# The opening of a two-layer trunk: where the first norm's sums are added up, and in which order the first steps stand

## The chip, the core and the metric

The kernel runs on one core of a Trainium2 chip. The metric is the device time of one execution in microseconds (us), lower is better. A core has five engines that run side by side, each through its own list of instructions: TensorE (PE; its weight loads are shown apart, as PEld), VectorE (DVE), ScalarE (ACT), GpSimd (POOL) and SyncE (SP), which here only issues DMA transfers. TensorE multiplies a stationary operand, loaded first, by a moving one, and adds up in PSUM banks; the other operands lie in SBUF.

## The reference, cut to what matters

The program is a trunk of two layers over 256 latent tokens and 256 context tokens of width 1024. Layer 0 has attention (a differential and a grouped-query part) and a gated feed-forward part, layer 1 a state-space mixer and a feed-forward part. The change touches only the way into layer 0:

```python
def rms_norm(x, g):
    x32 = x.astype(jnp.float32)
    y = x32 * lax.rsqrt(jnp.mean(x32 * x32, axis=-1, keepdims=True) + NORM_EPS)
    return (y * g.astype(jnp.float32)).astype(x.dtype)

def modulate(x, g, shift, scale):
    return rms_norm(x, g) * (1.0 + scale) + shift
...
        mod = jax.nn.silu(c) @ mod_w[layer] + mod_b[layer]
        mod_c = jax.nn.silu(c_ctx) @ mod_w[layer] + mod_b[layer]
        sh1, sc1, g1, sh2, sc2, g2 = jnp.split(mod[:, None, :], 6, axis=-1)
...
        h = modulate(x, norm_mix_g[layer], sh1, sc1)
        hc = modulate(ctx, norm_mix_g[layer], sh1c, sc1c)
...
    qa, ka, va, qb, kb, vb = jnp.split(h @ w_in, ATTN_SPLITS, axis=-1)
```

Before the first projection `h @ w_in` can start, the kernel needs one reciprocal root for each token and, for each channel, a shift and a scale out of the modulation `silu(c) @ mod_w`.

## The kernel before, in words

**Tiling.** Activations lie transposed: `self.x[k]`, k = 0 to 7, holds 128 channels by 512 tokens (256 latent, 256 context). Projections work in steps: `gemm_step` takes one 128x128 block of weights and issues three matmuls over 512 tokens, high part by high, high by low and low by high (L289, L290, L291), since both operands are split in two so as to keep fp32 accuracy. Weights come in units of eight blocks (512 KB); `take` hands out the next unit and `feed` keeps the loads going: `load_raw` (L244) issues the DMA on SP's queue into one of five `raw` buffers, and `split_one` copies the high part on ACT (L232) and subtracts it on POOL (for `ai`, the first projection) or DVE (L234) into one of two `ws` buffers. Modulation weights use the same `raw` buffers without a split. The order of all units is fixed by `plan`: at the start two halves of a modulation piece (`mod_s`), as many `ai` units as the next k needs, and so on. So a later load waits until an earlier unit has been used.

**The start.** SP issues the first parameters, the eight `x` pieces, constants, and then units. POOL writes constants (L622 to L632). ACT computes silu of the conditioning vectors (L635) into `cpad`, then runs a one-element Sqrt (L637), which brings that function's table in ahead of its use. In `attention`, PE first runs `spin`: matmuls over a zero tile whose results nobody reads, 30 of them. ACT squares each `x[k]` (L677); DVE and POOL add the eight squares up in two running sums (L680). `rstd_of` sums each of the two over channels on PE (`token_sums`, L504), adds the results on DVE (L542, L543), and `rsqrt` takes the reciprocal root with one correction step (L509 to L519). Between that and `spread` (L523), which copies each token's value over all partitions with matmuls, stands `fill`: the first modulation piece and spins.

**A modulation piece.** `mod_start(k, h)` multiplies one half of piece k (L451, four matmuls on four groups of 32 columns); `mod_fold(k)` copies the sums (L458), folds the four groups together on PE (L460) and writes shift and scale on DVE (L463, L465). `make_h(k)` then builds both halves of `h[k]`: the product on DVE (L561, tile `ht`), the high part on ACT (L563), the low part on DVE (L568).

**The loop behind it.** For each k, six blocks of `ai` are accumulated in six banks, and among them stand the two halves of piece k + 1, its fold, and `make_h(k + 1)`. At k = 0 the halves stand apart, with spins and one step between. Tile's scheduler orders the instructions of each engine, but those passed to `pin` (spins, modulation matmuls, folds, and here the spread) stay in program order among themselves. `SPIN` holds the numbers of spins at the seven places.

Of the kernel before, what the change touches and what calls it, by code (L numbers as in the profile page):

```python
# [11 lines left out]
F32 = mybir.dt.float32  # L12
BF16 = mybir.dt.bfloat16
F32R = mybir.dt.float32r
AF = mybir.ActivationFunctionType
ALU = mybir.AluOpType
# [4 lines left out]
P = 128  # L21
D = 1024
KD = 8
# [5 lines left out]
EPS = 1e-6  # L29
# [109 lines left out]
class Trunk:  # L139
# [124 lines left out]
    def drain(self):  # L264
        while self.queue:
            _, fn = self.queue.popleft()
            fn()


    def gemm_step(self, g):  # L270
# [314 lines left out]
    def normed_start(self, phase, g, n, l, cs):  # L585
        self.mod_flush()
        self.feed(self.n_use)
        ps = g.ps[0] = g.bank(f"{g.name}0")
        r = self.rows(self.rstd_of(self.nparts, n, D, fill=lambda: self.spin(ps, SPIN[5]), preload=AF.Gelu))
        self.spin(ps, SPIN[6])  # L590
        self.pinned = True
# [9 lines left out]
    def run(self):  # L601
        nc = self.nc
        self.plan()
        with self.pool("const") as cp, self.pool("small") as sp, self.pool("raw", bufs=RAW_BUFS) as rp, \
                self.pool("wsplit") as wp, self.pool("psum", space=PSUM) as pp:
            self.constp, self.smallp, self.rawp, self.splitp, self.psump = cp, sp, rp, wp, pp
            self.prm_t = cp.tile([P, NPRM], F32, name="prm")
            self.cst_t = cp.tile([P, 386], F32, name="cst")
            self.fold = self.cst_t[:, 384:386]
            self.ident = self.cst("ident")  # L610
            self.x = [cp.tile([P, 512], F32, name=f"x{k}") for k in range(KD)]
            self.h = [cp.tile([P, 2, 512], F32R, name=f"h{k}") for k in range(KD)]
            with self.tc.high_priority(PRIO):
                nc.sync.dma_start(out=self.prm_t[:, 0:128], in_=self.a["prm"][:, 0:128])
                for k in range(KD):
                    nc.sync.dma_start(out=self.x[k], in_=self.a["x"][k])
                nc.sync.dma_start(out=self.cst_t, in_=self.a["cst"][:, 0:386])
                for _ in range(3):
                    self.load_raw()
                nc.sync.dma_start(out=self.prm_t[:, 128:], in_=self.a["prm"][:, 128:])  # L620
            self.zero = cp.tile([P, P], BF16, name="zero")
            nc.gpsimd.memset(self.zero, 0.0)  # L622
            self.modT = [cp.tile([P, 48, 2], F32, name=f"modT{l}") for l in range(2)]
            self.cpad = cp.tile([P, KD, 32], F32, name="cpad")
            self.eps = cp.tile([P, 1], F32, name="eps")
            nc.gpsimd.memset(self.cpad, 0.0)
            nc.gpsimd.memset(self.eps, EPS)
            self.warm = cp.tile([P, 1], F32, name="warm")
            self.pick = cp.tile([P, 2, 32], F32, name="pick")
            nc.gpsimd.memset(self.pick, 0.0)  # L630
            for t in range(2):
                nc.gpsimd.memset(self.pick[:, t, t:t + 1], 1.0)  # L632
            self.modb1 = cp.tile([P, KD], F32, name="modb1")
            nc.vector.tensor_scalar(out=self.modb1, in0=self.prm("modb")[:, 8:16], scalar1=1.0, scalar2=None, op0=ALU.add)
            nc.scalar.activation(out=self.cpad[:, :, 0:2], in_=self.prm("c").rearrange("p (k t) -> p k t", t=2),  # L635
                                 func=AF.Silu)
            nc.scalar.activation(out=self.warm, in_=self.cpad[:, 0, 0:1], func=AF.Sqrt, scale=0.0, bias=self.eps)  # L637
            self.attention()
            self.ffn(0, 512, "f0i", "f0o")
            self.ssm()  # L640
            self.ffn(1, 256, "f1i", "f1o")
            self.final()


    def attention(self):
        nc, cp = self.nc, self.constp
        with self.pool("at") as ap:
# [21 lines left out]
            first = [self.bank(t, f"ai{m}") for m, t in enumerate(tags)]  # L669
            g.bank = lambda name: first.pop(0)  # L670
            self.mod_ps = self.bank("mod", "modps")
            self.spin(first[5], SPIN[0])
            acc = [ap.tile([P, 512], F32, tag="qf", bufs=3, name="xacc") for i in range(2)]
            for k in range(KD):
                sq = acc[k] if k < 2 else self.smallp.tile([P, 512], F32, tag="nacc" if k in (4, 7) else "sq",
                                                           bufs=1 if k in (4, 7) else 2, name="sq")
                nc.scalar.activation(out=sq, in_=self.x[k], func=AF.Square)  # L677
                if k >= 2:
                    o = k % 2 if k < 7 else 0
                    (nc.gpsimd if o else nc.vector).tensor_tensor(out=acc[o], in0=acc[o], in1=sq, op=ALU.add)  # L680

            def fill():
                for h in range(2):
                    self.mod_start(0, h)
                self.spin(first[5], SPIN[1])
                self.mod_fold(0)
                self.spin(first[5], SPIN[2])

            ps = self.rows(self.rstd_of(acc[::-1], 512, D, True, fill))
            self.spin(first[5], SPIN[3])  # L690
            self.make_h(0, (0, 1), 0, 1, ps)
            for k in range(KD):
                while len(g.held) * UB < 6 * (k + 1) - g.pos - (-g.pos) % UB:
                    g.held.append(self.take())
                if k + 1 < KD:
                    self.mod_start(k + 1, 0)
                    if k == 0:
                        self.spin(first[5], SPIN[4])
                        self.gemm_step(g)
                    self.mod_start(k + 1, 1)  # L700
                    for _ in range(2):
                        self.gemm_step(g)
                    self.mod_fold(k + 1)
                    self.make_h(k + 1, (0, 1), 0, 1, ps)
                while g.pos < 6 * k + 6:
                    self.gemm_step(g)
# [594 lines left out]
PRIO2 = 10  # L1301
FIRST = 7
LAM_AT = 6
SPIN = (30, 4, 0, 4, 2, 4, 4)
RAW_BUFS = 5
RAW_AHEAD = 3
SPLIT_BUFS = 2
# [91 lines left out]
```

## Time and profile before

| | |
|---|---|
| time, median of 3 runs | 1190.23 us (1189.91 to 1192.31) |
| the profiled execution's own time | 1190.27 us |
| its span, first to last instruction | 1188.5 us |
| PE busy | 1160.5 us, 98% of the span |
| DVE / ACT / POOL busy | 826.6 / 604.1 / 88.9 us |
| mean granted TensorE clock | 0.987 |
| first `ai` matmul (L289) | 21.55 us after the start |

Times in the views are us from the first instruction. In a timeline row stand start, duration, engine, line, operation, what it writes and reads, and how many were merged into the row; in brackets the idle time before it and what ended it. In the chain of waits a row is a piece of the chain that ended last. In a row of stretches stand its bounds, its length, PE's busy time and number of instructions, the granted clock as a share of full speed, the share of DMA time, and GB/s. A busy PE is not PE at its peak: a matmul over two columns is shown as busy while weights for the next are loaded.

### The profile page before, as it was taken

To read this page: it belongs to the slowest core of one execution; us is meant where nothing else is said; L and a number is where in the kernel's file an instruction comes from. 1 tells how busy PE (TensorE), PEld (TensorE's weight loads), DVE (VectorE), ACT (ScalarE), POOL (GpSimd) and SP (SyncE) were. 2 spreads that over 40 slices of the span, in tenths; PEclk is the share of its full clock that TensorE was granted. 3 is DMA by queue.
4 is the path that set the end of the run, shared out by engine and by line. 5 is a ranking of instruction groups with operands and counts; after the bars stand their busy time and mean duration, and the time that the engine had idled before them with its cause. 6 is when DMAs were issued, how large, how long until landed. Compare 5 with 4: busy or idle time off the path is not lost.

```text
span 1188.5 us, 17744 instructions
## 1 busy us (share of the span) xinstructions
PE 1160.5 (98%) x6902; PEld 950.5 (80%) x6902; DVE 826.6 (70%) x1341; ACT 604.1 (51%) x1072; POOL 88.9 (7%) x67
## 2 busy tenths in 40 slices
PE   8999999999999999999999998899999999999997
PEld 4765566668988888888888997787878898999997
DVE  3569756744767786855566468799999767877654
ACT  3266656543633333333223276777877546555542
POOL 2332112200000000000000000011111101000000
PEclk8999999999999999999999998899999999999998
DMA  8633133332255454644576232554545356776651
GB/s 294 236 132 107 53 107 107 107 107 79 81 155 165 140 186 135 188 131 146 179 242 230 73 105 96 147 146 119 141 127 125 104 183 188 234 216 217 184 182 54
DMA packets 56932, 176.67 MB, mean 149 GB/s; under 512 B 6096, under 2 KB 15888, under 8 KB 56848
## 3 DMA queue, kind: packets, MB, share of 16 engines
q1 hardware_dynamic: 56272, 175.01, 47.5%
q8 instruction: 54, 0.88, 0.3%
q10 hardware_dynamic: 576, 0.52, 0.1%
q14 instruction: 30, 0.25, 0.1%
HBM read 174.40 MB, written 1.11 MB: 148 GB/s over the span
## 4 chain that ended last, share of the span: by engine, by line
PE 88%; DVE 7%; ACT 2%; DMA 2%; issue 1%; POOL 0%; DVEq 0%; SPq 0%; ACTq 0%; POOLq 0%
PE f0i L289 6%; PE f0i L290 6%; PE f0i L291 6%; PE si L289 4%; PE f1i L290 4%; PE f1i L291 4%; PE f1i L289 4%; PE si L291 3%; PE si L290 3%; PE f0o L289 3%; PE f0o L290 3%; PE f0o L291 3%; PE ai L289 3%; PE ai L291 2%; PE ai L290 2%; PE y L1255 2%
## 5 line engine op out<-in xcount | busy, mean ns | idle before, releaser
L232 ACT ACTIVATE ws<-raw 128x1024 fp32r<-128x1024 f32 x215 | 227.1, 1056 | 264.8 <-PE f0i L291 91.3
L234 DVE TENSOR_TENSOR ws<-raw,ws 128x1024 fp32r<-128x1024 f32 x197 | 240.7, 1222 | 101.8 <-ACT ws L232 100.4
L289 PE MATMUL f0i<-h,ws 128*128 128x512 f32 x336 | 131.4, 391 | 0.0
L290 PE MATMUL f0i<-h,ws 128*128 128x512 f32 x336 | 130.9, 389 | 0.0
L291 PE MATMUL f0i<-h,ws 128*128 128x512 f32 x336 | 130.8, 389 | 0.0
L289 PE MATMUL si<-h,ws 128*128 128x256 f32 (+1 forms) x312 | 112.0, 359 | 3.7 <-DVE cacc L1019 3.7
L409 DVE SCALAR_TENSOR_TENSOR macc<-raw,cpad,macc 128x1024 f32<-128x1024 f32 x70 | 89.2, 1281 | 32.8 <-DMA raw<-mod_w 32.6
L291 PE MATMUL si<-h,ws 128*128 128x256 f32 (+1 forms) x312 | 107.0, 343 | 0.5 <-DVE ws L234 0.4
L290 PE MATMUL si<-h,ws 128*128 128x256 f32 (+1 forms) x312 | 106.6, 342 | 0.0
L290 PE MATMUL f1i<-h,ws 128*128 128x256 f32 x352 | 99.6, 283 | 0.3 <-DVE h L568 0.3
L289 PE MATMUL f1i<-h,ws 128*128 128x256 f32 x352 | 99.4, 284 | 0.3 <-ACT h L563 0.3
L291 PE MATMUL f1i<-h,ws 128*128 128x256 f32 x352 | 99.5, 283 | 0.0
L289 PEld LDWEIGHTS f0i<-h,ws 128*128 128x128 f32 x336 | 63.1, 188 | 14.3 <-ACT hid L573 0.8
L291 PEld LDWEIGHTS f0i<-h,ws 128*128 128x128 f32 x336 | 63.1, 188 | 13.2
L290 PEld LDWEIGHTS f0i<-h,ws 128*128 128x128 f32 x336 | 63.1, 188 | 12.8
L289 PEld LDWEIGHTS si<-h,ws 128*128 128x128 f32 x312 | 60.6, 194 | 14.8 <-issue 9.3
L289 PEld LDWEIGHTS f1i<-h,ws 128*128 128x128 f32 x352 | 67.3, 192 | 1.2 <-ACT h L563 0.7
L290 PEld LDWEIGHTS f1i<-h,ws 128*128 128x128 f32 x352 | 67.6, 192 | 0.5 <-DVE h L568 0.5
L291 PEld LDWEIGHTS f1i<-h,ws 128*128 128x128 f32 x352 | 67.6, 192 | 0.0
L291 PEld LDWEIGHTS si<-h,ws 128*128 128x128 f32 x312 | 60.4, 193 | 7.4 <-DVE ws L234 1.1
L290 PEld LDWEIGHTS si<-h,ws 128*128 128x128 f32 x312 | 60.7, 195 | 5.5
L289 PE MATMUL ai<-h,ws 128*128 128x512 f32 x144 | 62.5, 436 | 0.1
(293 smaller groups left out, 2668.4 us busy)
## 6 DMA issues: line engine op xcount, KB each, us to landing
raw<-mod_w SPq DMA_DIRECT2D x80, 512.0 KB, 3.7
raw<-w_f0i SPq DMA_DIRECT2D x44, 512.0 KB, 4.1
raw<-w_f1i SPq DMA_DIRECT2D x44, 512.0 KB, 4.2
raw<-w_si SPq DMA_DIRECT2D x41, 512.0 KB, 3.7
raw<-w_f0o SPq DMA_DIRECT2D x22, 512.0 KB, 4.6
raw<-w_f1o SPq DMA_DIRECT2D x22, 512.0 KB, 3.6
raw<-w_ai SPq DMA_DIRECT2D x18, 512.0 KB, 3.9
raw<-mod_s SPq DMA_DIRECT2D x16, 512.0 KB, 4.7
```

The source lines that it names most:

```text
L232: ops = [nc.scalar.activation(out=hi, in_=r, func=AF.Copy)]
L234: ops.append(eng.tensor_tensor(out=s[:, 1].rearrange("p a b -> p (a b)"), in0=r, in1=hi.bitcast(F32), op=ALU.subtract))
L289: nc.tensor.matmul(ps, lhsT=s[:, 0, b], rhs=xh[:, 0:n], start=first, stop=False)
L290: nc.tensor.matmul(ps, lhsT=s[:, 0, b], rhs=xl[:, 0:n], start=False, stop=False)
L291: nc.tensor.matmul(ps, lhsT=s[:, 1, b], rhs=xh[:, 0:n], start=False, stop=last)
L409: nc.vector.scalar_tensor_tensor(out=acc, in0=raw, scalar=sc, in1=acc, op0=ALU.mult, op1=ALU.add)
L1255: nc.tensor.matmul(y[c, 0:T], lhsT=lhs, rhs=rhs, start=(n == 0), stop=(n == 3))
```

## The change

The change rewrites the way up to the first `make_h`.

- A new function `first_norm` replaces the adds, `rstd_of` and `fill`. Each square goes into one of three `qf` buffers, and four matmuls with that square as the stationary operand and a two-column tile of ones (`one2`) as the moving one add it to eight columns of the modulation's bank, all eight squares into the same columns; a matmul over zeros opens the accumulation. One spin follows each square.
- Then come `rsqrt` on the accumulated sums, four spins, `spread`, and only behind it both halves of modulation piece 0, its fold, and three spins.
- A one-element Silu stands first on ACT, reading `eps`, so that table is asked for before the first parameters are there. The memsets of `eps` and `one2` stand ahead of that of `cpad`.
- At k = 0 two projection steps come first, then the two halves of piece 1 in a row, then one step, then the fold.
- The first spins are 12 in place of 30.

```diff
--- before.py
+++ after.py
@@ -265,6 +265,28 @@
         while self.queue:
             _, fn = self.queue.popleft()
             fn()
+
+    def first_norm(self, idle):
+        nc = self.nc
+        bank = self.bank("aux", "nsum")
+        sums = self.mod_ps[:, 504:512]
+        nc.tensor.matmul(sums, lhsT=self.zero, rhs=self.zero[:, 0:8], start=True, stop=False)
+        for k in range(KD):
+            sq = self.ap.tile([P, 512], F32, tag="qf", bufs=3, name="sqx")
+            nc.scalar.activation(out=sq, in_=self.x[k], func=AF.Square)
+            for q in range(4):
+                self.pin(nc.tensor.matmul(sums[:, 2 * q:2 * q + 2], lhsT=sq[:, P * q:P * q + P], rhs=self.one2,
+                                          start=False, stop=(k == KD - 1 and q == 3)))
+            self.spin(idle, SPIN[1])
+        r = self.smallp.tile([P, 4], F32, tag="rstd", name="rstd")
+        self.rsqrt(r, sums[:, 0::2], D, True)
+        self.spin(idle, SPIN[2])
+        self.spread(bank, r, 512, True)
+        for h in range(2):
+            self.mod_start(0, h)
+        self.mod_fold(0)
+        self.spin(idle, SPIN[4])
+        return bank
 
 
     def gemm_step(self, g):
@@ -623,9 +645,12 @@
             self.modT = [cp.tile([P, 48, 2], F32, name=f"modT{l}") for l in range(2)]
             self.cpad = cp.tile([P, KD, 32], F32, name="cpad")
             self.eps = cp.tile([P, 1], F32, name="eps")
+            self.warm = cp.tile([P, 1], F32, name="warm")
+            self.one2 = cp.tile([P, 2], F32, name="one2")
+            nc.gpsimd.memset(self.eps, EPS)
+            nc.scalar.activation(out=self.warm, in_=self.eps, func=AF.Silu)
+            nc.gpsimd.memset(self.one2, 1.0)
             nc.gpsimd.memset(self.cpad, 0.0)
-            nc.gpsimd.memset(self.eps, EPS)
-            self.warm = cp.tile([P, 1], F32, name="warm")
             self.pick = cp.tile([P, 2, 32], F32, name="pick")
             nc.gpsimd.memset(self.pick, 0.0)
             for t in range(2):
@@ -670,35 +695,17 @@
             g.bank = lambda name: first.pop(0)
             self.mod_ps = self.bank("mod", "modps")
             self.spin(first[5], SPIN[0])
-            acc = [ap.tile([P, 512], F32, tag="qf", bufs=3, name="xacc") for i in range(2)]
-            for k in range(KD):
-                sq = acc[k] if k < 2 else self.smallp.tile([P, 512], F32, tag="nacc" if k in (4, 7) else "sq",
-                                                           bufs=1 if k in (4, 7) else 2, name="sq")
-                nc.scalar.activation(out=sq, in_=self.x[k], func=AF.Square)
-                if k >= 2:
-                    o = k % 2 if k < 7 else 0
-                    (nc.gpsimd if o else nc.vector).tensor_tensor(out=acc[o], in0=acc[o], in1=sq, op=ALU.add)
-
-            def fill():
-                for h in range(2):
-                    self.mod_start(0, h)
-                self.spin(first[5], SPIN[1])
-                self.mod_fold(0)
-                self.spin(first[5], SPIN[2])
-
-            ps = self.rows(self.rstd_of(acc[::-1], 512, D, True, fill))
-            self.spin(first[5], SPIN[3])
+            ps = self.rows(self.first_norm(first[5]))
             self.make_h(0, (0, 1), 0, 1, ps)
             for k in range(KD):
                 while len(g.held) * UB < 6 * (k + 1) - g.pos - (-g.pos) % UB:
                     g.held.append(self.take())
                 if k + 1 < KD:
-                    self.mod_start(k + 1, 0)
-                    if k == 0:
-                        self.spin(first[5], SPIN[4])
+                    for _ in range(2 if k == 0 else 0):
                         self.gemm_step(g)
-                    self.mod_start(k + 1, 1)
-                    for _ in range(2):
+                    for h in range(2):
+                        self.mod_start(k + 1, h)
+                    for _ in range(1 if k == 0 else 2):
                         self.gemm_step(g)
                     self.mod_fold(k + 1)
                     self.make_h(k + 1, (0, 1), 0, 1, ps)
@@ -1301,7 +1308,7 @@
 PRIO2 = 10
 FIRST = 7
 LAM_AT = 6
-SPIN = (30, 4, 0, 4, 2, 4, 4)
+SPIN = (12, 1, 4, 0, 3, 4, 4)
 RAW_BUFS = 5
 RAW_AHEAD = 3
 SPLIT_BUFS = 2
```

## The prediction

> **What bounds the kernel now.** I read the page first, then the chain of waits, then the timeline of the first 40 us, then the granted clock.
>
> ```profile
> span 1188.5 us, 17744 instructions
> PE 1160.5 (98%) x6902; PEld 950.5 (80%) x6902; DVE 826.6 (70%) x1341; ACT 604.1 (51%) x1072; POOL 88.9 (7%) x67
> PE 88%; DVE 7%; ACT 2%; DMA 2%; issue 1%; POOL 0%; DVEq 0%; SPq 0%; ACTq 0%; POOLq 0%
> ```
>
> TensorE is the bound from end to end, so whatever time the first projection matmul (`ai`, L289) wins or loses should reach the end nearly one for one. The chain of waits before that matmul:
>
> ```profile
> 2.68 1.28 ACT L635
> ...
> 12.30 1.05 PE nsum L504 x8
> ...
> 14.71 1.82 PE ai L470 x4
> ...
> 17.18 1.92 PE nsum L523 x8
> 19.09 1.71 PE ai L470 x4
> ```
>
> Before 12.30 the chain runs through the silu table load, the squares and their adds (L680); behind it, through PE alone: sums, modulation piece, spins, fold, spread, spins. The timeline has the single steps (start, duration):
>
> ```profile
> 0.99 7.93 PE L470 MATMUL ai<-zero 128*128 128x512 bf16 x30 [0.99 <-POOL zero L622]
> ...
> 3.53 4.90 PEld L470 LDWEIGHTS <-zero 128*128 128x128 bf16 x23 [0.28 <-issue]
> ...
> 4.10 0.61 ACT L677 ACTIVATE xacc<-x 128x512 f32<-128x512 f32 x1
> 4.73 1.28 ACT L637 ACT_TABLE_LOAD   x1
> 6.03 0.30 ACT L637 ACTIVATE warm<-cpad,eps 128x1 f32<-128x1 f32 x1
> ...
> 13.29 1.43 PE L451 MATMUL modps<-raw,cpad 128*32 128x256 f32 x16
> 13.40 0.16 DVE L542 COPY nsa<-nsum 128x4 f32<-128x4 f32 x1 [1.15 <-PE nsum L504]
> ...
> 13.78 0.30 ACT L509 ACTIVATE rstd<-nsb,eps 128x4 f32<-128x4 f32 x1 [3.34 <-DVE nsb L543]
> ...
> 14.92 0.16 DVE L519 TENSOR_TENSOR rstd<-rstd,nt 128x4 f32<-128x4 f32 x1
> ...
> 19.13 0.87 DVE L561 SCALAR_TENSOR_TENSOR ht<-x,modT,nsum 128x256 f32<-128x256 f32 x2 [1.44 <-PE nsum L523]
> ...
> 20.19 0.88 DVE L568 SCALAR_TENSOR_TENSOR h<-ht,modT,h 128x256 fp32r<-128x256 f32 x2 [0.18 <-ACT h L563]
> ...
> 21.55 0.59 PE L289 MATMUL ai<-h,ws 128*128 128x512 f32 x1
> ...
> 24.60 0.50 PE L460 MATMUL modps<-cst,modsb 128*128 128x2 f32 x4
> ...
> 25.46 0.86 DVE L561 SCALAR_TENSOR_TENSOR ht<-x,modT,nsum 128x256 f32<-128x256 f32 x2
> ...
> 27.18 0.16 PEld L451 LDWEIGHTS modps<-raw,cpad 128*32 128x32 f32 x8 [0.35 <-DVE h L568]
> ...
> 33.30 1.07 PE L451 MATMUL modps<-raw,cpad 128*32 128x256 f32 x16
> ...
> 34.44 0.42 DVE L458 COPY modsb<-modps 128x256 f32<-128x256 f32 x1
> ```
>
> The mark to beat is 21.55. The granted clock (PE busy and its instructions, then PEclk) changes at steps of 3.41 us:
>
> ```profile
> 7.04:10.46 3.42, 1.89 (x9) 1.00 1.04 390
> 10.46:13.87 3.41, 2.62 (x28) 1.00 1.03 416
> 13.87:17.28 3.41, 3.41 (x21) 0.50 1.01 394
> 17.28:20.70 3.42, 3.42 (x12) 0.50 0.86 309
> ...
> 61.66:65.07 3.41, 1.95 (x10) 1.00 0.31 126
> 65.07:68.48 3.41, 3.41 (x9) 0.50 0.45 154
> ```
>
> The column to watch is which instructions were busy. Nine spins (1.89 us) kept the clock in 7.04 to 10.46. The stretch 10.46 to 13.87 looked busier (2.62), but held two-column sums and part of a modulation piece, and the clock was halved behind it. So loads of weights with two columns behind them seem not to count; wide matmuls do. (The first six spins, from 0.99 to 3.53, took 0.42 each, and the later ones 0.21: they ran at half speed too.)
>
> **The change, part by part.** *Sums on TensorE.* Six adds of the squares go (L680, on DVE and POOL), and two small DVE steps, L542 and L543: from 13.40 to 13.78, 0.38 us on the path. In their place each of eight squares gets four matmuls, eight PE records; eight took 0.99 us at full clock (12.30 to the next start at 13.29). With one spin (4.90/23 = 0.21) behind them a square costs 0.99 to 1.20; I take 1.1, as part of the next load hides under the spin. At half clock I take 2.2, near the eight loads of L523 in 1.92 plus a spin.
>
> ```profile
> L616 SPq DMA_DIRECT2D x<-x x8: 421/432/433, 1.2 to 4.5; - x8
> DMA to landing us min/median/max: 2.9/4.0/4.9
> ```
>
> The x pieces land from 1.2 + 2.9 = 4.1 to at most 9.4, one in 0.75 us: PE at 1.1 a square, not ScalarE at 0.6, sets the pace. Now ScalarE's squares wait for PE, through their three buffers; behind ScalarE nothing else is due then.
>
> *Silu table at once.* The table load moves into the wait for the first parameters, so that silu, which waited for it until 2.68 + 1.28, ends 1.3 earlier, about 2.9. If the Sqrt table follows directly (1.28 + 0.30), the first square ends at 5.1; if it stays behind the first square, that ends at 4.7 but the second only at 6.84, and the later sums slip by 0.7. The trace cannot say which: I add half, 0.35. The two memsets placed ahead of the others on POOL cost 0.1 us each, hidden, since silu needs `cpad` only at 2.6.
>
> *Spins 30 to 12.* Six at 0.42 and six at 0.21 end at 4.9, before the first square. In 3.63 to 7.04 wide work is 1.2 plus one or two 0.21: near 1.5 us, against 1.89 kept and at most ten of 0.21 to 0.23 in 61.66 to 65.07, two of them two-column ones, lost: so under 1.8. I let the clock stand there. In 7.04 to 10.46 there are three spins, 0.64: the clock falls at 10.46.
>
> *Sum of the start.* First sums 5.1; five squares done by 10.6; three at 2.2, less the last spin: sums done 16.8, where now it is 13.36. Then five spins (2.1, to 18.9) cover the norm (13.78 to 15.08 now, so 18.4). Spread, 1.9: 20.8. At 20.70 the clock returns, as that stretch was full of spins and spread. The modulation piece now stands behind the spread: 16 matmuls and copy, 33.30 to 34.86 = 1.56: 22.4. Fold to `ht`, 24.60 to 25.46: 23.3. `ht` to the first projection matmul, hi alone being ready, 1.6 of the 1.9 that the pair of L561 to the end of L568 takes: 24.9. That is 3.3 later than 21.55.
>
> *Halves joined, two steps first.* At 21.55 half of the next piece (0.54, half of the 1.07 at 33.30) was already done; now all of it follows. Against that, the 0.35 wait at 27.18 goes, since the later fold still has three steps behind it that cover `make_h`. Net +0.2.
>
> *Clock at 24.1.* In 20.70 to 24.11 stand the piece and three spins, 1.5 us of wide work: undecided. Ends 0 and (27.5 - 24.9)/2 = 1.3; no row separates them, so half, 0.65.
>
> *Queues.* SP's loads of the second `w_ai` unit and of the next `mod_s` halves wait for raw buffers that the moved piece frees:
>
> ```profile
> 13.99 0.33 SPq L244 DMA_DIRECT2D raw<-w_ai  x1
> ...
> 20.46 1.04 ACT L232 ACTIVATE ws<-raw 128x1024 fp32r<-128x1024 f32 x1
> ...
> 21.58 2.39 POOL L234 TENSOR_TENSOR ws<-raw,ws 128x1024 fp32r<-128x1024 f32 x1 [4.13 <-ACT ws L232]
> ```
>
> ```profile
> DMA to landing us min/median/max: 3.4/4.4/7.8
> ```
>
> 13.99 becomes about 21.4. At the longest landing, 7.8, and with its split (1.04 + 2.39) the unit is ready at 32.7. It is due at the ninth step: eight steps of three matmuls at 0.23, two pieces of 1.07 and a fold of 0.50 behind 24.9, so at 33.1. Hence 0; if the cover is gone, what lands late is paid in full, at most some 3 us with the queues' own delay. The halves of `mod_s` come next on SP and are due at about 30, against 22 + 4.4 = 26.4.
>
> *Later on.* At k = 7 PE waits for `h`, then loses the clock:
>
> ```profile
> 62.60 2.30 DVE h L568
> ```
>
> ```profile
> PE ai L290 <- DVE h L568: 1.4, 1, 1.4
> ```
>
> That wait filled most of one clock stretch. Moved by 4.5 us it straddles the edge at 68.48, and neither side falls short: the half-clock 65.07 to 68.48 goes, -1.7. The wait itself stays.
>
> Sum: 3.3 + 0.35 + 0.2 + 0.65 - 1.7 = +2.8 us. The profiled execution took 1190.27 for a span of 1188.5, 1.77 around it, and stands 0.04 above the median of 1190.23. Forecast: 1191.3 + 1.77 = 1193.0.
>
> [...]
>
> **Rivals.** *The clock holds* (faster side). If loads count as activity, eight squares at 1.1 end at 13.95. Norm 1.3, spread at half of 1.92, piece and copy 1.56, fold 0.9, then 1.6: first matmul at 20.3, 1.2 early. With +0.2, +0.35 and half of the -1.7 (at this smaller shift the later wait may still fill its stretch), -1.5: 1188.7; with all of the 1.7 and the table ahead of the first square, 1187.5. It decides if the clock stays 1.00 past 13.9. For it: the order is right for a warm PE, with spread and piece back to back. Against: 10.46 to 13.87.
>
> *The clock falls already at 7.04.* Two squares done by 7.3, six at 2.2 less a spin: 20.0; spins 22.1, spread 24.0, piece and copy 25.6, fold 26.5, first matmul 28.1: +6.5, +0.2, +0.65, -1.7 = +5.7: 1195.9. For it: 1.5 us of wide work is below every stretch seen kept here.
>
> *Nothing comes of it in sum.* The late start costs as forecast, but at k = 7 the copy of weights on ScalarE no longer slips between the two halves of `h`, so the 1.4 us wait goes as well and the 24.1 stretch stays warm: 2.8 - 1.4 - 0.65 = +0.8: 1191.0. Speaks for it: one ordering of instructions there causes it. Against: nothing of that order is touched.
>
> **Chances.** Forecast 0.45 (own range 1190.5 to 1195), clock holds 0.33, falls at 7.04 0.12, nothing 0.10. A difference of 0.2%, 2.4 us, is about what this measurement can tell. Slower: 0.6 of the forecast and all of the third, 0.39. Faster: half of the second (below 1187.8 only with most of its open terms) and a third of the last, 0.20. Same: the rest, 0.41. Below 1187.2 or above 1196.6 lie the warm case with another gain at k = 7 and the earliest fall with a cold start.
>
> **What would show it.** PEclk 0.50 from about 10.5 to 20.7 and L504 pieces of 1.9 us behind it confirm the sums; the first `ai` matmul near 24.9 confirms the sum, near 20.3 the rival. The spread must start before the first L451, L542 and L543 must be gone, and a full clock should show from 65 to 69. I am wrong if loads keep the clock up, if ScalarE's order delays the first square, or if the order of later work changes with the start.

## The result, and the profile after

The changed kernel took 1199.48 us (median of four, 1198.62 to 1200.73) beside 1190.07 us for the kernel before (four, 1189.44 to 1192.31): a ratio of 1.0085, interval [1.0066, 1.0104]. It is slower by 9.4 us; forecast was 2.8. Every ratio here is estimated from all runs of both kernels, so it need not be the quotient of the two medians. The profiled execution took 1200.73 us, on its page:

```profile
span 1198.9 us, 17806 instructions
PE 1173.6 (98%) x6938; PEld 955.9 (80%) x6938; DVE 822.5 (69%) x1335; ACT 604.7 (50%) x1073; POOL 86.0 (7%) x66
```

The span is 10.4 us longer and TensorE's busy time 13.1, so the loss lies on TensorE and not in a wait for DVE, ACT or POOL, which have nearly the same or less to do.

First the view of stretches, cut at the same places of the program in both kernels: from the start to the first matmul of `f0i` (layer 0's first feed-forward projection), from there to its end, then to the start of `f1i` (the same projection of layer 1), then to the end. Columns: bounds, length, PE busy and instructions, granted clock, DMA share, GB/s. Before (the last two rows are `f1i` and `f1o` alone, for later):

```profile
0.00:311.72 311.72, 302.70 (x1625) 0.98 0.39 129
311.72:557.52 245.80, 245.80 (x1169) 1.00 0.48 151
557.52:986.71 429.19, 418.25 (x2507) 0.98 0.50 146
986.71:1188.50 201.79, 193.72 (x1606) 0.98 0.59 181
986.71:1115.19 128.48, 128.19 (x1068) 1.00 0.68 210
1115.19:1178.55 63.36, 63.36 (x532) 1.00 0.44 134
```

After:

```profile
0.00:319.07 319.07, 311.60 (x1660) 0.97 0.38 126
319.07:571.10 252.03, 252.03 (x1169) 1.00 0.48 148
571.10:998.94 427.84, 417.72 (x2506) 0.99 0.49 146
998.94:1198.90 199.96, 192.25 (x1608) 0.98 0.59 182
```

Row by row the differences are +7.35, +6.23, -1.35 and -1.83 us: +10.4. In the third row the clock was halved for 9.3 us in place of 13.7, by the places of its edges, worth up to 2.2 us at half speed, for the 1.35. The second row is the surprise. The change touches nothing there, TensorE has the same 1169 instructions, is busy all of the time, and runs at full clock in both, yet it needs 6.2 us more. The groups of instructions by line, which give the mean duration in ns as the last number of the busy part, show that each matmul is longer. Before:

```profile
L289 PE MATMUL f0i<-h,ws 128*128 128x512 f32 x336 | 131.4, 391 | 0.0
...
L289 PE MATMUL f1i<-h,ws 128*128 128x256 f32 x352 | 99.4, 284 | 0.3 <-ACT h L563 0.3
```

After (L311 is the old L289):

```profile
L311 PE MATMUL f0i<-h,ws 128*128 128x512 f32 x336 | 133.4, 397 | 0.0
...
L311 PE MATMUL f1i<-h,ws 128*128 128x256 f32 x352 | 99.2, 283 | 0.0
```

Six ns on each of 3 x 336 matmuls are 6 us. `f1i` is shorter by 1 to 2 ns a matmul: it lasts 126.74 us for 128.48, nearly the whole of the fourth row.

The first row is the opening. Its timeline after the change (L492 are spins, L662 the load of the Sqrt table, L276 squares, L278 the sums, L545 the spread, L473 the modulation piece, L311 the projection):

```profile
0.99 5.30 PE L492 MATMUL ai<-zero 128*128 128x512 bf16 x12 [0.99 <-POOL one L652]
...
2.98 1.28 ACT L662 ACT_TABLE_LOAD   x1
...
7.47 0.95 PE L278 MATMUL modps<-one,sqx 128*128 128x2 f32 x8
...
8.51 0.63 ACT L276 ACTIVATE sqx<-x 128x512 f32<-128x512 f32 x1 [0.39 <-PE modps L278]
...
11.01 1.71 PE L278 MATMUL modps<-one,sqx 128*128 128x2 f32 x8
...
18.41 2.29 PE L492 MATMUL ai<-zero 128*128 128x512 bf16 x5
...
20.50 1.91 PE L545 MATMUL nsum<-cst,rstd 128*128 128x128 f32 x8
22.35 1.70 PE L473 MATMUL modps<-raw,cpad 128*32 128x256 f32 x16
...
27.03 1.64 PE L311 MATMUL ai<-h,ws 128*128 128x512 f32 x3 [1.16 <-ACT h L585]
```

A square's eight records take 0.95 us from 7.47 until about 10 us and 1.71 from 11.01 on; from the fourth square on, ACT waits for PE, not the other way round. The first projection matmul starts at 27.03, where it was 21.55. The longer sums go with the granted clock (the number behind PE's instructions in the row):

```profile
3.19:6.60 3.41, 3.41 (x12) 1.00 1.03 327
6.60:10.01 3.41, 3.41 (x32) 1.00 1.03 385
10.01:13.43 3.42, 3.42 (x18) 0.50 1.02 413
...
20.25:23.66 3.41, 3.41 (x26) 0.50 0.02 5
23.66:27.08 3.42, 1.70 (x16) 1.00 0.74 226
27.08:30.49 3.41, 3.41 (x11) 0.50 0.61 234
```

The stretch from 6.60 to 10.01 holds sums and one spin a square. PE is shown busy all of it, and behind it the clock is halved until 23.66. (The rows up to 6.60 show the clock as 1.00 too, but all twelve spins took 0.42 us each, which is half speed: nothing is recorded before the first edge.) The next stretch holds 1.70 us of PE, and the clock is halved once more, over the first projection steps.

### The profile page after: what moved, and what is told of

It reads as the page before. It is cut to its first block, busy times and chain, and to the rows that moved or that the text cites. A ratio compares the mean times of both kernels' runs of the same rounds, so it can differ in the third digit from the quotient of the medians.

```text
span 1198.9 us, 17806 instructions
## 1 busy us (share of the span) xinstructions
PE 1173.6 (98%) x6938; PEld 955.9 (80%) x6938; DVE 822.5 (69%) x1335; ACT 604.7 (50%) x1073; POOL 86.0 (7%) x66
## 4 chain that ended last, share of the span: by engine, by line
PE 91%; DVE 6%; ACT 1%; DMA 1%; issue 1%; POOL 0%; DVEq 0%; ACTq 0%; POOLq 0%
PE f0i L311 7%; PE f0i L313 7%; PE f0i L312 7%; PE si L311 4%; PE si L313 4%; PE si L312 4%; PE f1i L311 4%; PE f1i L312 3%; PE f1i L313 3%; PE f0o L311 3%; PE f0o L313 3%; PE f0o L312 3%; PE ai L311 3%; PE ai L312 3%; PE ai L313 3%; PE y L1262 2%
## 5 line engine op out<-in xcount | busy, mean ns | idle before, releaser
L311 PE MATMUL f0i<-h,ws 128*128 128x512 f32 x336 | 133.4, 397 | 0.0
L313 PE MATMUL f0i<-h,ws 128*128 128x512 f32 x336 | 132.9, 396 | 0.0
L312 PE MATMUL f0i<-h,ws 128*128 128x512 f32 x336 | 132.9, 395 | 0.0
L311 PE MATMUL si<-h,ws 128*128 128x256 f32 (+1 forms) x312 | 111.3, 357 | 3.7 <-DVE cacc L1026 3.7
L311 PE MATMUL f1i<-h,ws 128*128 128x256 f32 x352 | 99.2, 283 | 0.0
L311 PEld LDWEIGHTS f0i<-h,ws 128*128 128x128 f32 x336 | 63.1, 188 | 16.2 <-issue 1.2
L313 PEld LDWEIGHTS f0i<-h,ws 128*128 128x128 f32 x336 | 63.1, 188 | 15.3
L311 PEld LDWEIGHTS si<-h,ws 128*128 128x128 f32 x312 | 59.4, 190 | 15.2 <-issue 9.3
L311 PEld LDWEIGHTS f1i<-h,ws 128*128 128x128 f32 x352 | 66.6, 190 | 0.8 <-ACT hid L595 0.4
L313 PEld LDWEIGHTS f1i<-h,ws 128*128 128x128 f32 x352 | 66.3, 188 | 0.0
L312 PEld LDWEIGHTS f1i<-h,ws 128*128 128x128 f32 x352 | 66.3, 188 | 0.0
L313 PEld LDWEIGHTS si<-h,ws 128*128 128x128 f32 x312 | 59.4, 190 | 7.5 <-DVE ws L234 0.7
L312 PEld LDWEIGHTS si<-h,ws 128*128 128x128 f32 x312 | 59.6, 191 | 6.0
L311 PE MATMUL ai<-h,ws 128*128 128x512 f32 x144 | 63.0, 443 | 1.2 <-ACT h L585 1.2
```

Of the source, the lines that this page charges most:

```text
L311: nc.tensor.matmul(ps, lhsT=s[:, 0, b], rhs=xh[:, 0:n], start=first, stop=False)
L312: nc.tensor.matmul(ps, lhsT=s[:, 0, b], rhs=xl[:, 0:n], start=False, stop=False)
L313: nc.tensor.matmul(ps, lhsT=s[:, 1, b], rhs=xh[:, 0:n], start=False, stop=last)
```

## Experiments

Two questions stood open: why `f0i` is longer, and how much of the opening's loss is the clock's. For the first, the theory was place: the new two-column tile `one2` takes 32 bytes ahead of the buffers of the weights, so `ws` and everything behind it moves by 32 bytes, while `h` stays where it was (so the compiled programs place them). The rival was that something of the changed opening carries on: other timing of transfers, other order of instructions.

**The tile alone (e1).** The kernel before, with a tile that is written once and never read:

```diff
             self.warm = cp.tile([P, 1], F32, name="warm")
+            self.idle2 = cp.tile([P, 2], F32, name="idle2")
+            nc.gpsimd.memset(self.idle2, 1.0)
```

> The kernel before with one idle tile of two columns of ones placed where the change places its own, and nothing else. Theory (placement): the tile moves every buffer that is allocated behind it, the weights ws among them, by 32 bytes against the activations h, and that sets the pace of the matmuls: f0i steps go from 227 to 234 ns each (+6 us in f0i), f1i from 120 to 117 ns (-1.8 us), the opening stays (first ai matmul near 21.6 us), in sum +3 to +5 us. Rival (order): the slower f0i comes from the order of instructions or from transfers that the later start shifts; then this kernel stays within 1 us of the kernel before, at 227 and 120 ns.

Measured: 1192.34 us against 1188.61 for the kernel before beside it, ratio 1.0044 [1.0027, 1.0060]. The first projection matmul starts at 21.54, as before. `f0i`, in the view of stretches:

```profile
312.46:564.52 252.06, 252.06 (x1169) 1.00 0.49 148
```

252.06 us, the length it has in the changed kernel; its matmuls take 397 ns (L289), those of `f1i` 282. So an unread tile of two columns costs nearly half of what the whole change costs, and place is what does it, or at least nothing that the opening does. The same run holds a control. The matmuls of `f0o`, layer 0's second feed-forward projection, are 512 columns wide too, but their moving operand `hid` lies behind the tile as `ws` does, so that both move. They keep their pace; before, then e1:

```profile
L289 PE MATMUL f0o<-hid,ws 128*128 128x512 f32 x154 | 60.5, 393 | 0.0
...
L289 PE MATMUL f0o<-hid,ws 128*128 128x512 f32 x154 | 60.6, 394 | 0.0
```

Nor does the slower pace come from what else is going on: from one 512-column matmul of `f0i` to the next are 226.9 ns before and 233.3 in e1, and in e1 it is 233.4 alike while ACT writes a weights' buffer, while DVE writes one, while ACT, DVE and POOL all do nothing, and while no DMA runs.

**The change without the tile (e2).** The ones are read out of `pick`, which the kernel has anyway, as a view with a step:

```diff
-            self.one2 = cp.tile([P, 2], F32, name="one2")
...
-            nc.gpsimd.memset(self.one2, 1.0)
...
+            self.one2 = self.pick.rearrange("p a b -> p (a b)")[:, 0:34:33]
```

> The changed kernel without its own tile of ones: the two columns of ones are a strided view of a constant that is there anyway, so that all buffers lie where they lay before the change. Placement theory: f0i back at 227 ns, f1i back at 120 ns, the opening as slow as in the changed kernel (first ai matmul 26 to 28 us), 1194 to 1196 us. Rival (order): as slow as the changed kernel, 1198 to 1201 us, with f0i at 234 ns.

Measured: 1195.69, ratio 1.0058 [1.0042, 1.0074]. `f0i`:

```profile
318.27:564.37 246.10, 246.10 (x1169) 1.00 0.49 151
```

It is back to 246; the first projection matmul still starts at 26.77. The two halves of the loss come apart: 0.58% stays with the opening.

**The changed kernel once more (e0).** It ran beside these, so that parts and whole share a chip.

> The changed kernel once more, on the same chip as the two kernels beside it. Expected 1198 to 1201 us under either theory, f0i at 234 ns and f1i at 117 ns; the edges of the clock's 3.41 us stretches may lie elsewhere, and with them the first ai matmul between 25 and 28 us.

Measured: 1201.32, ratio 1.0097 [1.0076, 1.0118]. The difference to e2, 0.39%, is the tile's share within the change, within the noise of the 0.44% that it costs alone. In this profiled execution the clock first rose at 4.20 instead of 6.60, fell at 11.03 and returned at 21.27. The sums were done at 15.3 and the first projection matmul started at 24.17: the same program, 2.9 us apart, and the two timelines part where the clock does. The opening of the kernel before has such a spread too: left as it was in e1, e8 to e10 and e12 to e14, it starts the projection between 19.93 (e14) and 21.54 (e1), so that 21.55 is its late end.

**Four spins behind each square (e3).** On top of e2, to test the clock:

```diff
-SPIN = (12, 1, 4, 0, 3, 4, 4)
+SPIN = (12, 4, 4, 0, 3, 4, 4)
```

> As the changed kernel without its tile, with four spins behind each square in place of one. Theory (clock): what slows the sums is the halved clock, which falls because the two-column sums do not count as work. With 0.85 us of wide matmuls in each 1.7 us the granted clock stays 1.00 through the sums, a square costs about 1.7 us, and the matmuls of sums take 0.95 us for eight throughout instead of 1.71. First ai matmul 24 to 27 us although 24 spins are added. Rival (loads): the weight loads themselves slow down in a row, whatever the clock; then the pieces take 1.7 us again, a square costs 2.5 us or more and the first ai matmul comes near 32 us.

Measured: 1193.09, ratio 1.0038 [1.0021, 1.0056]: 2.6 us less than e2, with 24 spins more. The view of stretches:

```profile
9.12:12.53 3.41, 3.41 (x26) 1.00 1.02 412
12.53:15.95 3.42, 3.42 (x26) 1.00 0.99 397
```

Here, too, PE is shown busy for all of each stretch, and the clock stays. What differs from 6.60 to 10.01 above is what it is busy with: 26 records, of which some eight are 512-column spins, against 32 of which three are. The sums keep their 0.95 us to the end, and in the timeline the spread falls from 1.91 to 1.05:

```profile
20.24 1.05 PE L545 MATMUL nsum<-cst,rstd 128*128 128x128 f32 x8
...
25.28 0.96 PE L311 MATMUL ai<-h,ws 128*128 128x512 f32 x3 [1.16 <-ACT h L585]
```

Yet even warm, the projection starts 3.7 us late, since the spins that keep the clock make a square cost 1.67 us, and eight of those are slower than the adds on DVE and POOL were: the sums end at 18.5, where they ended at 13.36. One spin a square loses the clock, four lose the time; two and three were not tried. That e3 is faster than e2 is likely and not certain, as their intervals overlap.

**Single parts, on the kernel before.** Each of these leaves out the tile.

Sums on TensorE with one spin each and 12 spins ahead, order as before behind them (e7):

```diff
-            acc = [ap.tile([P, 512], F32, tag="qf", bufs=3, name="xacc") for i in range(2)]
...
+            sums = self.mod_ps[:, 504:512]
+            nc.tensor.matmul(sums, lhsT=self.zero, rhs=self.zero[:, 0:8], start=True, stop=False)
             for k in range(KD):
...
-                    (nc.gpsimd if o else nc.vector).tensor_tensor(out=acc[o], in0=acc[o], in1=sq, op=ALU.add)
+                for q in range(4):
+                    self.pin(nc.tensor.matmul(sums[:, 2 * q:2 * q + 2], lhsT=sq[:, P * q:P * q + P], rhs=self.one2,
+                                              start=False, stop=(k == KD - 1 and q == 3)))
+                self.spin(first[5], 1)
...
-SPIN = (30, 4, 0, 4, 2, 4, 4)
+SPIN = (12, 4, 0, 4, 2, 4, 4)
```

> The kernel before with one part of the change: the sums of squares accumulate on TensorE with one spin behind each square and 12 spins at the start, the two columns of ones a view of a constant (no buffer moves), everything behind the sums as before. Theory (clock and sums): the granted clock falls between 9 and 11.5 us, the sums end at 17 to 19 us, the first ai matmul comes at 25 to 28 us, +4 to +7 us: nearly the whole loss of the opening. Rival (order): the loss is in the norm ahead of the modulation; then the first ai matmul comes below 24 us.

Measured: 1195.62 against 1190.19, ratio 1.0043 [1.0024, 1.0061]. The clock is half from 7.52 to 24.58, and the first projection matmul starts 6.3 us late:

```profile
27.87 0.58 PE L289 MATMUL ai<-h,ws 128*128 128x512 f32 x1
```

That is no less than the 5.5 us by which the whole change starts late: most of the opening's loss comes with this part, 0.43% beside the 0.58% of e2.

The halves of piece 1 joined behind two projection steps (e4):

```diff
-                    self.mod_start(k + 1, 0)
-                    if k == 0:
-                        self.spin(first[5], SPIN[4])
+                    for _ in range(2 if k == 0 else 0):
                         self.gemm_step(g)
-                    self.mod_start(k + 1, 1)
-                    for _ in range(2):
+                    for h in range(2):
+                        self.mod_start(k + 1, h)
+                    for _ in range(1 if k == 0 else 2):
                         self.gemm_step(g)
```

> The kernel before with one part of the change: at k = 0 two projection steps, then both halves of piece 1, one step, the fold, and no spins among them. Theory (the loss is the sums and the tile): this part costs nothing or gives a little; first ai matmul 20.7 to 21.1 us instead of 21.55, since neither half a piece nor spins stand ahead of it, and from the second k on -0.5 to +0.3 us. Rival (the joined halves starve the fold): the 30th ai matmul comes 0.5 us or more later than before.

Measured: 1191.20, ratio 1.0008 [0.9993, 1.0024]. The first projection matmul starts at 20.18, inside the spread of the unchanged opening, and the 40th is 0.6 us early. That is lost again at k = 7, where the clock was half for two stretches in a row in this execution, and for one in the kernel before:

```profile
65.05:68.46 3.41, 3.41 (x13) 0.50 0.39 149
68.46:71.88 3.42, 3.42 (x10) 0.50 0.00 0
```

The silu table at once (e5):

```diff
+            self.warm = cp.tile([P, 1], F32, name="warm")
+            nc.gpsimd.memset(self.eps, EPS)
+            nc.scalar.activation(out=self.warm, in_=self.eps, func=AF.Silu)
             nc.gpsimd.memset(self.cpad, 0.0)
-            nc.gpsimd.memset(self.eps, EPS)
-            self.warm = cp.tile([P, 1], F32, name="warm")
```

> The kernel before with one part of the change: the one-element Silu ahead of everything on ScalarE. Theory: squares and their adds move up by the 1.3 us of the table load that now lies in the wait for the parameters, as far as the x pieces have landed; sums done 12.4 to 13.0 instead of 13.36 us, first ai matmul 20.6 to 21.3 us; 0 to -1 us in the end. Rival: the x pieces or the adds on POOL and DVE set the pace and nothing moves, within 0.2 us of 13.36.

Measured: 1191.33, ratio 1.0005 [0.9987, 1.0024]. Both table loads move ahead as they should, and the time that this frees goes into a wait for the next piece of `x`:

```profile
7.73 3.28 ACT L678 ACTIVATE sq<-x 128x512 f32<-128x512 f32 x5 [1.45 <-DMA x<-x]
```

The sums start at 11.44 in this execution and at 10.96 in the kernel before: here the squares waited for `x`, not for the table. But `x` also landed later in this execution (median 5.2 us behind its issue, 4.0 in the kernel before), and the clock was half from 12.36 to 22.60, so that the first projection matmul came at 23.37, 1.8 us late and not early. What the table's place is worth by itself is therefore not shown.

The norm ahead of the modulation (e6):

```diff
-            def fill():
...
-            ps = self.rows(self.rstd_of(acc[::-1], 512, D, True, fill))
+            ps = self.rows(self.rstd_of(acc[::-1], 512, D, True, lambda: self.spin(first[5], SPIN[1])))
+            for h in range(2):
+                self.mod_start(0, h)
+            self.mod_fold(0)
```

> The kernel before with one part of the change: its squares are added on DVE and POOL as before, but the spread stands ahead of both halves of piece 0 and its fold, with four spins ahead of it and four behind the fold. Theory: the order by itself costs, as the piece, its copy and its fold (some 3 us) now follow the spread instead of filling the wait for the norm; first ai matmul 21.8 to 23 us, +0.3 to +1.5 us. Rival: the order gains, because the spread no longer waits for the spins and the fold; first ai matmul below 21.3 us.

Measured: 1191.39, ratio 1.0009 [0.9997, 1.0022]; the first projection matmul 1.1 us late, nothing left of that at `f0i`. The parts by their ratios: tile 0.44%, sums 0.43%, norm ahead 0.09%, joined 0.08%, silu 0.05%: 1.09%. That lies within the whole's interval in e0, 0.76 to 1.18%, and just above that of the first measurement, 0.66 to 1.04%. The last three cannot be told from nothing.

**What it is about the place.** The tile put ahead of `h` instead, so that `h` and `ws` both move by 32 bytes (e9):

```diff
+            self.idle2 = cp.tile([P, 2], F32, name="idle2")
             self.h = [cp.tile([P, 2, 512], F32R, name=f"h{k}") for k in range(KD)]
+            nc.gpsimd.memset(self.idle2, 1.0)
```

> The kernel before with the idle tile of 8 bytes allocated ahead of h, so that h and ws both move by 32 bytes. Theory (place of one against the other): f0i at 227 ns and f1i at 120 ns, time within 1.5 us of the kernel before. Rival (the place of ws by itself, or of the raw buffers that the transfers fill): f0i at 234 ns and f1i at 117 ns as in the tile-only run, +3 to +5 us.

Measured: 1190.14 against 1190.23, ratio 0.9997 [0.9981, 1.0012]; `f0i` matmuls are at 391 ns again. The stretch:

```profile
309.91:556.81 246.90, 246.41 (x1169) 1.00 0.50 150
```

The same tile costs nothing here (half a microsecond of the stretch is a wait for weights): what counts is the place of the weights against that of `h`. That also excludes the tile's memset as the cause.

A tile of 64 bytes (e8) and one of 128 bytes (e14, 32 columns), where the tile of e1 stood, tested whether a distance comes back at a round number:

```diff
+            self.idle16 = cp.tile([P, 16], F32, name="idle16")
+            nc.gpsimd.memset(self.idle16, 1.0)
```

> The kernel before with an idle tile as in the tile-only run, but 64 bytes wide, so that weights ws move by 64 bytes against the activations h instead of 32. Theory (place modulo 64): the pace is set by whether ws and h start in the same or in opposite halves of 64 bytes; back in the same half, f0i runs at 227 ns and f1i at 120 ns, and the time is that of the kernel before within 1.5 us. Rival (any move of ws costs): f0i at 234 ns or another value, +3 us or more.

> The kernel before with an idle tile of 128 bytes in place of the 8 bytes of the tile-only run. Theory (a cycle of 128 bytes): f0i back at 227 ns and f1i at 120 ns. Rival (any move of the weights against the activations costs the 512-column matmuls and helps the 256-column ones): f0i at 231 to 236 ns, f1i at 117 ns or below.

Measured: e8 1192.89 against 1190.23, ratio 1.0024 [1.0005, 1.0044]; e14, one execution, 1194.62 against 1191.48. The groups of instructions of e8:

```profile
L289 PE MATMUL f0i<-h,ws 128*128 128x512 f32 x336 | 133.5, 397 | 0.0
...
L289 PE MATMUL f1i<-h,ws 128*128 128x256 f32 x352 | 97.4, 278 | 0.3 <-ACT h L563 0.3
```

Of e14, where `f0i` reads 396 (L289):

```profile
L289 PE MATMUL f1i<-h,ws 128*128 128x256 f32 x352 | 100.5, 287 | 0.0
```

At 32, 64 and 128 bytes the 512-column matmuls of `f0i` pay the same 5 to 6 ns, and no round distance brought them back. Those of `f1i`, 256 columns, went from 284 to 282, 278 and 287. That the cost comes and goes with 64 or 128 bytes is excluded for `f0i`. For `f1i` it is not: the stage lasts 128.5 us without a tile, 126.8, 123.2 and 128.5 with 32, 64 and 128 bytes, so that at 128 bytes it is back where it was. The rule is not found.

**A better version out of it.** If the place sets the pace, `f1i` can be given a better one by moving layer 1's moving operands. The columns of `h` and of `hid` in its feed-forward part start `o` elements later (e10, o = 8, 32 bytes):

```diff
+    ho = 0
...
-            hi, lo = self.h[k][:, 0, c], self.h[k][:, 1, c]
+            d = slice(c.start + self.ho, c.stop + self.ho)
+            hi, lo = self.h[k][:, 0, d], self.h[k][:, 1, d]
...
-            hid = [fp.tile([P, 2, n], F32R, name=f"hid{f}") for f in range(KF)]
+            o = self.ho = 8 if l else 0
+            hid = [fp.tile([P, 2, n + 2 * o], F32R, name=f"hid{f}")[:, :, o:o + n] for f in range(KF)]
...
-            g.x = lambda k: (self.h[k][:, 0], self.h[k][:, 1])
+            g.x = lambda k: (self.h[k][:, 0, o:], self.h[k][:, 1, o:])
```

The weights move with them, however: each of the 22 `hid` buffers grows by 128 bytes, and layer 1's `ws` buffers lie behind them, 2816 bytes further (5632 in e12 and 8448 in e13, in the compiled programs). So these runs show that place matters in layer 1 as well, but not what a distance of 32, 64 or 96 bytes by itself does.

> The kernel before, with h and the hidden activations of the second feed-forward part placed 32 bytes off ws (their 256 columns start at column 8), all else in its place: the first feed-forward part keeps the same half of 64 bytes, which its 512-column matmuls like, and the second gets the opposite half, which the 256-column ones seem to like. Theory: f0i stays at 227 ns, f1i goes from 120 to 117 ns (-1.8 us) and f1o from 120 to 117 ns (-1.6 us); -2.5 to -3.5 us in sum. Rival: f1i stays at 120 ns, since what moved it was ws and not the pair; no change.

Measured: 1187.99 against 1190.23, ratio 0.9978 [0.9959, 0.9997], with `f0i` at 391 and `f1i` at 281, 279 and 279 ns; `f1i` lasts 125.05 us. With the joined halves of e4 as well (e11):

> As the placed kernel, with the one part of the change that brought the start forward in its own run: at k = 0 two steps, both halves of piece 1, one step, the fold, no spins among them. Theory: the first ai matmul comes 0.5 to 1.4 us earlier than in the placed kernel at the same place of the clock's edges, the 60th 0.6 us earlier, and the time is 0 to 1 us below that of the placed kernel. Rival: as in the run of this part alone, the half-clock stretches that follow eat it up; the same time or up to 1.5 us above.

Measured: 1187.54, ratio 0.9980 [0.9966, 0.9993]: the same as e10, so the joined halves add nothing. With o = 16, 64 bytes (e12):

> As the placed kernel, with h and the hidden activations of the second feed-forward part starting at column 16, 64 bytes off the weights, instead of column 8. Theory (distance, the same in both directions): f1i goes to 113 ns as with the 64-byte tile, f1o below 117.5 ns, f0i stays at 227 ns; 5 to 8 us under the kernel before and 2 to 5 us under the placed kernel. Rival (it is the direction, or the place of ws by itself): f1i at 117 ns or more; no better than the placed kernel.

Measured: 1185.28 against 1191.48, ratio 0.9958 [0.9941, 0.9975], the lowest ratio of all and faster than both kernels, though its interval overlaps that of e10. Its `f0i`, `f1i` and `f1o`:

```profile
308.81:554.79 245.98, 245.98 (x1169) 1.00 0.49 151
985.23:1111.92 126.69, 126.69 (x1070) 0.99 0.69 213
1111.92:1174.11 62.19, 62.19 (x531) 1.00 0.46 137
```

Beside 245.80, 128.48 and 63.36 before: `f1i` gains 1.8 us and `f1o` 1.2. That is 3.0 of the some 5 us; the rest was not separated from where the clock's edges fell. In `f1i` e12 is slower than e10 (126.69 us for 125.05), so that it is not shown to be the better of the two. Its matmuls there came to 280 to 282 ns, not to the 277 or 278 of e8. With o = 24, 96 bytes (e13), in one execution:

> As the placed kernel, with the activations of the second feed-forward part starting at column 24, 96 bytes off. Theory (the further off within a stretch of 128 bytes or more, the faster at 256 columns): f1i at 113 ns or below. Rival (a cycle of 128 bytes about 64): f1i back at 117 ns, as with 32.

Measured: 1191.58 against 1191.48, with `f1i` at 286, 283 and 281 ns: as far as one execution shows, the gain is gone.

## Why the prediction was wrong

The direction and the first mechanism, a clock that falls over the sums, were right; the time, 1193.0 forecast and 1199.48 measured, fell outside the range. No rival has a term for place. For the opening, the rival with the early fall came nearest: full clock for one stretch only, as here from 6.60 to 10.01, and a first projection matmul at 28.1, for 27.03 measured. Against the forecast of +2.8 the profiled execution has +10.4. The 7.6 between them lie, by the four rows of stretches, at +4.6 in the first (7.35 against 2.8), +6.2 in the second, and -3.2 in the last two, for which nothing was forecast. By single `ai` matmuls the changed kernel is 5.5 us late at the first, 7.4 at the 30th, 8.2 at the 60th, 6.8 at the 140th and 8.4 at the 200th.

**The step that failed: the memset of the new tile, priced as "0.1 us each, hidden".** As an instruction it is that. As a buffer it moved `ws` against `h`, and that is the largest single term that the forecast missed: e1 shows 252.06 for 245.80 us in `f0i` with nothing else changed. The prediction listed each instruction and each queue, and had no line for where buffers lie. The same move gave 1.7 us back in `f1i` (126.74 after, 128.48 before).

**The step that was sized too small: the start.** The forecast took the clock's edges of one profile as given. It had half of the twelve spins warm, and so ending at 4.9; all twelve ran cold and ended at 6.1. It had the sums done at 16.8 and the first projection matmul at 24.9; these came at 18.4 and 27.03, behind a half clock of 13.65 us (10.01 to 23.66) where 10.24 was forecast. In e0's execution, with the first rise at 4.20 and not at 6.60, they came at 15.3 and 24.17, on the other side of the forecast. That is the forecast's own course, two stretches of full clock and then half. Over the profiled executions of all kernels here the first rise lay between 3.63 (before) and 7.02 us (e4), 3.4 us apart, and the later edges follow at multiples of 3.41 us. So the start was never one number: two executions of one program lie nearly 3 us apart, and which of the two would be measured was luck.

**The stretch behind the start**, undecided in the forecast at 0.65, lost its clock in full: 27.08 to 30.49 in the changed kernel, 24.68 to 28.09 in e0's execution, some 1.7 us, as half of 3.41. The row ahead of it held 1.70 us of PE, from 23.66 to 27.08.

**What held.** One spin a square does not keep the clock, and weight loads with two columns behind them do not hold it up: 6.60 to 10.01 has PE busy throughout (3.41 of 3.41 us), and the clock falls behind it to 0.50, while e3, with four spins a square, keeps it at 1.00 (9.12 to 15.95). PE and not ScalarE sets the pace of the squares, at 1.02 us warm (7.47 to the next at 8.50) and 1.95 cold (11.01 to 12.96), where 1.1 and 2.2 were forecast. The spread stands ahead of the piece, the two small DVE steps are gone, and the Sqrt table followed silu directly, so that of the 0.35 for it nothing was due. And the loads moved behind the piece were hidden: the second `w_ai` unit was asked for at 23.49, 2.1 later than forecast, and from 27 to 60 us no matmul waited for weights.

**Right by luck: the 1.7 us at k = 7.** The half clock from 65 to 68 went, and the lead of the kernel before shrinks from 8.2 to 6.8 us there, but not as forecast. The wait stayed 1.4 us. It had not filled most of its stretch (1.95 of 3.41 us were busy), and it did not come to straddle an edge: it lies from 71.91 to 73.27, again within one stretch of the changed kernel, which kept the clock.

```profile
71.45:74.87 3.42, 2.06 (x9) 1.00 0.23 56
...
73.27 0.50 PE L312 MATMUL ai<-h,ws 128*128 128x512 f32 x1 [1.36 <-DVE h L590]
```

Another half clock, from 95.34 to 98.76, took the lead back up to 8.4. The stretch ahead of it had PE busy for 3.25 of 3.42 us, some 2.3 of them with 512-column matmuls (0.8 of these over 64 rows only), more than the 2.06 that kept the clock above. So which work counts for the clock is not settled by the width of the matmuls alone.

## What to carry to other kernels

Price a new buffer by what it moves as well as by what writes it: compare the mean duration of the untouched matmuls and the length of their stage, stage by stage, ahead of any explanation by the code that was changed. Where TensorE is kept warm by filler, price a chain of small matmuls for both places of the clock's edges, since one profile shows only one (the changed kernel's clock first rose at 6.60 us in one execution, at 4.20 in another). And work that another engine does while TensorE only spins is not yet a reason to move it: the adds on DVE and POOL were on the path, but they were done at 12.3, and on TensorE the sums ended between 15.3 (e0) and 20.8 (e7), depending on the clock they had.

## What was not expected of the hardware

In these runs the pace of TensorE's matmuls changed with where the stationary and the moving operand lie to each other, in steps as small as 32 bytes: 391 or 397 ns for the 512 columns of `f0i`, at a granted clock of 1.00 and with no wait in either kernel, and 278 (e8) to 287 ns (e14) for the 256 columns of `f1i`. Moving both together changed nothing (`f0i` at 391 ns in e9, `f0o` at 393 before and 394 in e1). The two widths went different ways: with `ws` 32 bytes further, `f0i` lasts 2.5% longer (252.03 for 245.80 us) and `f1i` is 1.4% shorter (126.74 for 128.48). That other engines' writes or the DMA do it is excluded by the 233.4 ns without the ones and without the other; by what mechanism the place sets the pace, no run shows. Which rule of addresses stands behind it is open: 32, 64 and 128 bytes cost `f0i` the same 5 to 6 ns, while `f1i` is back at its old length, 128.5 us, with 128.
